# A fused QKV projection on one core: the first two row pairs dealt on even and odd rows, and the first pair's x loaded as two transfers

## The chip, the cores and the metric

The kernel runs on one core of one Trainium2 chip. The metric is device time in microseconds (us). Three runs of the kernel before gave 358.24, 358.25 and 358.67 us; their median is 358.25 us. One more execution was profiled: it took 358.3 us, and the profile covers a span of 356.5 us of it.

The engines are named as in the profile: PE is TensorE (PEld its weight loads), DVE is VectorE, ACT is ScalarE, POOL is GpSimd and SP is SyncE, which here issues most of the DMA transfers. A "q" behind a name (SPq) is that engine's sequencer.

## The reference

```python
batch, seq, hidden = 16, 512, 768
x      # (16, 512, 768)  float32
w_qkv  # (768, 2304)     float32

qkv = np.matmul(x, w_qkv)                   # (16, 512, 2304)
q, k, v = qkv[..., :768], qkv[..., 768:1536], qkv[..., 1536:]
return np.stack([q, k, v], axis=0)          # (3, 16, 512, 768)
```

Flattened, this is an 8192 x 768 matrix times a 768 x 2304 matrix, with the 2304 columns of the product cut into three outputs. 25 MB of x and 7 MB of weights are read, and 75.5 MB are written.

## The kernel before, in words

**Tiling.** The 8192 rows of x are worked through in 32 *pairs*; pair `p` holds rows 256p to 256p+255, as two row tiles of 128 rows each. The 768 inner elements are six slices `j` of 128 (`KT = 6`). The 2304 columns are two wide groups `q` of 1024 columns, each of two blocks `c` of `CB = 512`, and a remainder of 256 columns between them (`REM`). A row of x or of an output is 768 floats, which is 3072 bytes.

**Two ways to multiply.** Pairs 2 to 31 use a seven-product scheme (L234 to L291) on sums of x and sums of weights. Those sums of the weights are not there at the start, so the first two pairs (`ND = 2`) are multiplied in the plain way, in bf16, by `block` (L463 to L489), which walks over the slices `j` and, within a slice, over the four row tiles of pairs 0 and 1. The change touches only these first two pairs.

**How pairs 0 and 1 are prepared.** `load_rows(p)` (L157) loads a whole pair in one DMA transfer of 768 KB: partition m receives row m of the first tile and row 128+m of the second. `cast_row` (L168) then casts one row tile to bf16, its columns split between DVE and ACT; `turn_row` (L173) transposes it on PE into PSUM; `copy_row` (L182) copies it out of PSUM into `xb`, from which the products take their stationary operand. All other pairs come in by other loads (L125 to L145) and are transposed on DVE.

**Order of the work.** The schedule is manual: each engine runs its instructions in the order in which the code lists them. The opening is L434 to L548. SP issues, one after another: the two x loads, six weight slices of 256 KB each for block (0, 0) (L441), two transfers of 768 KB for block (0, 1), the remainder's weights, eight transfers of 96 KB for pair 2, and so on. Eight DMA semaphores are handed out in turn, so each transfer's issue waits until the transfer eight places before it has landed: the first eight are issued without a wait, and the first 768 KB transfer of block (0, 1) waits for pair 0's load, the second for pair 1's load.

PE meanwhile runs ten matmuls on a tile of zeros (`busy(10)`, L521). Then come the transposes of pair 0, two more matmuls on zeros (L527), the transposes of pair 1, and the 24 products of block (0, 0) (L541). The casts stand in the same order on DVE and ACT: both row tiles of pair 0, both row tiles of pair 1, then the weight slices. On DVE the first copy out of PSUM stands between pair 0's casts and pair 1's.

**Stores.** `rows_of(s, p, lo, hi)` (L293) gives the place of a pair in output s. `store_quad` (L296) uses it for the wide groups and `rem` (L313) for the remainder. The stores of pairs 0 and 1 are issued from L581, L584 and L626.

Of the kernel before, what the change touches and what calls it, by code (L numbers as in the profile page):

```python
# [10 lines left out]
def kernel(  # L11
# [20 lines left out]
    nc = tc.nc  # L32
    P = 128
# [6 lines left out]
    KH = KT // 2  # L40
    KC = K // 4
    NP = M // (2 * P)
    CB = 512
    REM = N3 - 4 * CB
    Q_OFF = (0, 2 * CB + REM)
    R_OFF = 2 * CB
    fp32 = mybir.dt.float32
# [6 lines left out]
    x_flat = x.rearrange("b t h -> (b t) h")  # L54
    out_flat = out.rearrange("s b t h -> s (b t) h")
# [21 lines left out]

    b1 = [w_pool.tile([P, KT, CB], bf16, name=f"b1_{q}") for q in range(2)]
    b22 = [w_pool.tile([P, KH, CB], f32r, name=f"b22_{q}") for q in range(2)]
    t_0 = w_pool.tile([P, 4, KH, CB], f32r, name="t_0")  # L80
    w_rem[1] = rem_pool.tile([P, KH, REM], bf16, name="w_rem1")
# [39 lines left out]
    xin, xf, xb, sr = {}, {}, {}, {}  # L121
# [19 lines left out]
    def load_x(p, other):  # L141
        xin[p] = xin_pool.tile([P, 2 * P // G, KC], fp32, name="xin")
        load_x_half(p, 0, nc.sync)
        if other is not None:
            load_x_half(p, 1, other)  # L145

    def transpose(p, cuts=(0, 8)):
        if p not in xf:
            xf[p] = xf_pool.tile([P, KT, 2 * P], fp32, name="xf")
        turned = xf[p][:].rearrange("p j (g b) -> p g j b", b=G)  # L150
        rows = xin[p][:].rearrange("p g (a j) -> p g j a", a=G)
        for g, end in zip(cuts, cuts[1:]):
            nc.vector.transpose(turned[:, g:end], rows[:, g:end])  # L153

    def load_rows(p):  # L157
        xin[p] = xin_pool.tile([P, 2, K], fp32, name="xin")
        rows = x_flat[p * 2 * P:(p + 1) * 2 * P, :]
        nc.sync.dma_start(xin[p][:], rows.rearrange("(r m) k -> m r k", m=P))  # L160

    xc, turned_rows = {}, {}

# [63 lines left out]
    def quad(p, q, pool=o_pool, tag="o"):  # L227
        u = Quad()
        u.p, u.q = p, q
        u.o = pool.tile([P, 2, 2 * CB], fp32, name="o", tag=tag)  # L230
        u.x = u.y = u.z = None
        return u

    def product(u, n, ps, start):  # L234
        t1, t2, t3, t4 = ts[u.q]
        if n <= 2:
            h = (n - 1) * KH
            lhs = [xb[u.p][:, h + j, :P] for j in range(KH)]
            rhs = [b1[u.q][:, h + j, :] for j in range(KH)]
        else:  # L240
            k, t = {3: (4, b22[u.q][:]), 4: (0, t4), 5: (1, t1), 6: (2, t2), 7: (3, t3)}[n]
            lhs = [sr[u.p][:, k, j, :] for j in range(KH)]
            rhs = [t[:, j, :] for j in range(KH)]
        for j in range(KH):
            nc.tensor.matmul(  # L245
                ps[:], lhs[j], rhs[j],
                start=(start and j == 0), stop=(j == KH - 1), skip_group_check=True,
            )
# [7 lines left out]
    def do(u, n, out=True):  # L256
# [17 lines left out]
        elif n == 5:  # L274
            u.y = bank()
            product(u, 5, u.y, True)
            if u.p == NP - 1:
                nc.scalar.activation(c22, u.y[:], ident)
        elif n == 7:
            product(u, 7, u.x, False)  # L280
            if u.p == NP - 1:
                nc.vector.tensor_tensor(c22, c22, u.x[:], op=add)
# [8 lines left out]
            nc.vector.tensor_tensor(c12, c12, u.y[:], op=add)  # L291

    def rows_of(s, p, lo, hi):  # L293
        return out_flat[s, p * 2 * P:(p + 1) * 2 * P, lo:hi].rearrange("(r m) n -> m r n", m=P)

    def store_quad(u):  # L296
        if u.q == 0:
            nc.sync.dma_start(rows_of(0, u.p, 0, H), u.o[:, :, :H])
            nc.sync.dma_start(rows_of(1, u.p, 0, 2 * CB - H), u.o[:, :, H:])
        else:  # L300
            part = 2 * H - Q_OFF[1]
            nc.sync.dma_start(rows_of(1, u.p, H - part, H), u.o[:, :, :part])
            nc.sync.dma_start(rows_of(2, u.p, 0, H), u.o[:, :, part:])
# [9 lines left out]
    def rem(p, eng=nc.sync, between=None):  # L313
        ps = ps_pool.tile([P, 2, REM], fp32, name="ps")
        rem_row(p, 0, ps[:, 0, :])
        if between is not None:
            between()
        rem_row(p, 1, ps[:, 1, :])

        def copied():  # L320
            o = or_pool.tile([P, 2, REM], fp32, name="orem")
            act.activation(o[:], ps[:], ident)  # L322
            return lambda: eng.dma_start(rows_of(1, p, R_OFF - H, R_OFF - H + REM), o[:])

        return copied

    def two(a, b, early, u=None):

        do(a, 1)
        do(b, 1, u is None)  # L330
        if u is None:
            early()
            rem(a.p)()()
        else:
            middle(u)
            copied = rem(a.p, between=lambda: third(u))
            evacuate(b)
            early()
            copied()()
            fourth(u)  # L340
            load_x(a.p + 3, nc.sync)
        do(a, 2)
        do(b, 2)
        summed(a, b)
# [27 lines left out]
    def plain(a, b, c, d, early, rem_c, stored=False):  # L372

        add_first(a)
        add_first(b)
        rem(a.p)()()
        do(c, 1)
        do(d, 1)
        early()
        rem_c()  # L380
        do(c, 2)
        do(d, 2)
        add_second(a)
        add_second(b)
        if stored:
            for u in (c, d):
                store_cols(u, 0, 0, CB, nc.sync)
# [43 lines left out]
        rem_stored(a.p, 1, 2, lambda dst, src: act.activation(dst, src, ident), nc.sync)  # L431


    ND = 2  # L434
    zero = xb_pool.tile([P, CB], bf16, name="zero", tag="xb")
    nc.vector.memset(zero[:], 0.0)
    load_rows(0)
    nc.scalar.activation(tiny[:], zero[:, :1], ident)
    make_identity(nc, eye)
    load_rows(1)  # L440
    load_blocks(0, 0, 1)  # L441
    load_blocks(0, 1)
# [66 lines left out]
    def ahead(p, reversed_pair):  # L509
        transpose(p)  # L510
        if reversed_pair:
            sums_x(p)
            round_x(p)
        else:
            round_x(p)
            sums_x(p)
# [114 lines left out]
    def load_next(p, other):  # L631
        if p < NP:
            load_x(p, other)

    def early():
        ahead(ND + 2, False)
        load_x(ND + 3, nc.sync)

    two(quad(ND + 1, 0), quad(ND + 1, 1), early, u2)

    def early():
        ahead(ND + 3, True)
        load_x(ND + 5, nc.sync)

    two(quad(ND + 2, 0), quad(ND + 2, 1), early)
    transpose(ND + 4, (0, 4))

    for p in range(ND + 3, NP - 1, 2):
        first = p == ND + 3
# [6 lines left out]
        def early():  # L656
            ahead(p + 2, p + 2 < NP - 1)
            load_next(p + 4, nc.scalar)
# [6 lines left out]
        c, d = quad(p + 1, 0), quad(p + 1, 1)  # L665
        final = p + 3 >= NP
        plain(a, b, c, d, early, lambda: rem(c.p)()(), final)
# [32 lines left out]
```

## Time and profile before

| what | before |
|---|---|
| median of three runs | 358.25 us |
| the profiled execution | 358.3 us |
| its span | 356.5 us |
| PE busy | 351.5 us (99%) |
| DVE / ACT / POOL busy | 264.3 / 186.0 / 177.3 us |
| DMA moved | 108.10 MB, mean 303 GB/s |
| pair 0's x landed | 5.03 us after the start of the span |
| pair 1's x landed | 6.86 us |
| first product of block (0, 0) | 8.12 us |

The chain of waits is read backwards from the last instruction, and says at each step what the work had waited for. Idle time of an engine off that chain costs nothing. Times inside the profile are counted from the start of its span. A line of the timeline gives start, duration (of a merged group, from its first start to its last end or next start), engine, line, operation, tiles, shapes, how many, and in brackets the idle time before it with what ended it. The lines of the windows give, for one stretch, busy time and number of instructions of each engine, the granted PE clock, the DMA share, and GB/s.

### The profile page before, as it was taken

How to read it: one execution, taken by the hardware profiler on the slowest of the kernel's cores; microseconds unless marked ns; L12 is line 12 of the kernel's file. 1: busy time of each engine (PE TensorE's matmuls, PEld its weight loads, DVE VectorE, ACT ScalarE, POOL GpSimd, SP SyncE). 2: the span in 40 equal slices, each digit the busy share in tenths (PEclk: the TensorE clock that was granted, in tenths of full speed). 3: DMA queues.
4: the chain of work that ended last, by engine and by line, in shares of the span. 5: the costliest groups of instructions: out<-in, count | busy, mean ns of one | idle time of the engine just before them, and what ended most of it. 6: DMA issues, size and time to landing. Idle time of an engine off the chain costs nothing.

```text
span 356.5 us, 5348 instructions
## 1 busy us (share of the span) xinstructions
PE 351.5 (99%) x1782; PEld 252.2 (71%) x1782; DVE 264.3 (74%) x309; ACT 186.0 (52%) x321; POOL 177.3 (50%) x184
## 2 busy tenths in 40 slices
PE   7999999999999999999999999999999999999996
PEld 3474677768677686877768677686877868777675
DVE  3799876796877869777695876969777696876743
ACT  4587755445454553645545454553645545454553
POOL 0121773376566453665535566353665535566320
PEclk9999999999999999999999999999999999999999
DMA  7998999999999898998979889699999989887397
GB/s 297 379 351 258 323 373 344 371 325 360 293 337 311 250 362 204 357 258 299 351 189 385 229 311 338 174 406 242 346 272 299 331 196 390 232 295 293 146 377 273
DMA packets 82075, 108.10 MB, mean 303 GB/s; under 512 B 4992, under 2 KB 62080, under 8 KB 82048
## 3 DMA queue, kind: packets, MB, share of 16 engines
q1 hardware_dynamic: 75520, 103.04, 86.2%
q10 hardware_dynamic: 6528, 4.72, 5.1%
q8 instruction: 14, 0.23, 0.3%
q14 instruction: 13, 0.11, 0.1%
HBM read 32.24 MB, written 75.50 MB: 302 GB/s over the span
## 4 chain that ended last, share of the span: by engine, by line
PE 97%; DMA 2%; ACT 0%; SPq 0%; issue 0%
PE ps L245 79%; PE ps L308 11%; PE ps L479 6%; DMA xin<-in_x_dram 2%; PE ps L412 0%; PE ps L179 0%; ACT xc L166 0%; SPq L160 0%; ACT orem L431 0%
## 5 line engine op out<-in xcount | busy, mean ns | idle before, releaser
L245 PE MATMUL ps<-t,s 128*128 128x512 f32 x720 | 178.0, 395 | 0.0
L245 PEld LDWEIGHTS ps<-t,s 128*128 128x128 f32 x720 | 135.0, 188 | 29.6
L153 DVE STREAM_TRANSPOSE xf<-xin 128x768 f32<-128x768 f32 (+2 forms) x46 | 93.4, 2033 | 2.8 <-DMA xin<-in_x_dram 2.8
L245 PE MATMUL ps<-b,xb 128*128 128x512 bf16 x360 | 85.2, 379 | 0.0
L285 DVE TENSOR_TENSOR o<-o,ps 128x512 f32<-128x512 f32 x56 | 38.5, 687 | 51.8 <-ACT o L284 51.8
L192 POOL CAST xb<-xf 128x1536 bf16<-128x1536 f32 x28 | 41.0, 1465 | 56.9 <-DVE xf L153 56.9
L212 POOL TENSOR_TENSOR s<-xf 128x384 fp32r<-128x384 f32 x29 | 31.0, 1067 | 72.9 <-DVE xf L153 71.2
L245 PEld LDWEIGHTS <-xb 128*128 128x128 bf16 x360 | 34.0, 98 | 36.9 <-issue 4.2
L291 DVE TENSOR_TENSOR o<-o,ps 128x512 f32<-128x512 f32 x60 | 41.1, 686 | 20.7 <-PE ps L245 19.5
L284 ACT ACTIVATE o<-ps 128x512 f32<-128x512 f32 x56 | 33.5, 598 | 42.1 <-PE ps L245 42.1
L245 PE MATMUL ps<-b,s 128*128 128x512 f32 x180 | 50.6, 389 | 0.0
L288 ACT ACTIVATE o<-ps 128x512 f32<-128x512 f32 x60 | 35.9, 598 | 25.2 <-PE ps L245 22.8
L365 DVE TENSOR_TENSOR o<-o,ps 128x512 f32<-128x512 f32 x78 | 47.8, 681 | 0.0
L273 ACT ACTIVATE o<-ps 128x512 f32<-128x512 f32 x60 | 36.0, 599 | 19.1 <-PE ps L245 15.4
L308 PE MATMUL ps<-w_rem,xb 128*128 128x256 bf16 x372 | 45.7, 273 | 0.0
L322 ACT ACTIVATE orem<-ps 128x512 f32<-128x512 f32 x31 | 18.5, 597 | 49.1 <-PE ps L308 28.5
L308 PEld LDWEIGHTS <-xb 128*128 128x128 bf16 x372 | 36.2, 98 | 10.9 <-issue 0.3
L245 PEld LDWEIGHTS ps<-b,s 128*128 128x128 f32 x180 | 33.8, 188 | 7.0
L213 POOL TENSOR_TENSOR s<-s,xf 128x384 fp32r<-128x384 f32 x29 | 29.5, 1018 | 2.3
L214 POOL TENSOR_TENSOR s<-xf 128x384 fp32r<-128x384 f32 x29 | 29.4, 1015 | 0.0
L216 POOL TENSOR_TENSOR s<-xf,s 128x384 fp32r<-128x384 f32 x29 | 29.2, 1008 | 0.0
L369 ACT ACTIVATE o<-ps 128x512 f32<-128x512 f32 x26 | 15.5, 598 | 16.9 <-PE ps L245 16.1
(53 smaller groups left out, 164.9 us busy)
## 6 DMA issues: line engine op xcount, KB each, us to landing
out_dram<-o SPq DMA_DIRECT2D x60, 768.0 KB, 4.7
out_dram<-o SPq DMA_DIRECT2D x76, 256.0 KB, 3.9
xin<-in_x_dram SPq DMA_DIRECT2D x88, 192.0 KB, 5.6
out_dram<-orem SPq DMA_DIRECT2D x31, 256.0 KB, 2.4
xin<-in_x_dram ACTq DMA_DIRECT2D x24, 192.0 KB, 4.4
st<-in_w_qkv_dram SPq DMA_DIRECT2D x5, 768.0 KB, 7.7
xin<-in_x_dram SPq DMA_DIRECT2D x2, 768.0 KB, 4.9
st<-in_w_qkv_dram SPq DMA_DIRECT2D x6, 256.0 KB, 6.0
```

Source lines behind the costliest of these rows:

```text
L153: nc.vector.transpose(turned[:, g:end], rows[:, g:end])
L192: nc.gpsimd.tensor_copy(out=xb[p][:], in_=xf[p][:])
L212: 1: lambda g: g.tensor_tensor(s[:, 1], a21, a22, op=add),
L213: 2: lambda g: g.tensor_tensor(s[:, 2], s[:, 1], a11, op=sub),
L245: nc.tensor.matmul(ps[:], lhs[j], rhs[j], start=(start and j == 0), stop=(j == KH - 1), skip_group_check=True,)
L273: nc.scalar.activation(c12, u.x[:], ident)
L284: nc.scalar.activation(c22, u.x[:], ident)
L285: nc.vector.tensor_tensor(c22, c22, u.y[:], op=add)
L288: nc.scalar.activation(c21, u.x[:], ident)
L291: nc.vector.tensor_tensor(c12, c12, u.y[:], op=add)
L308: nc.tensor.matmul(ps, xb[p][:, j, r * P:(r + 1) * P], w_rem[j // KH][:, j % KH, :], start=(j == 0), stop=(j == KT - 1), skip_group_check= ...
L365: dve.tensor_tensor(c, c, u.z[:], op=add)
```

## The change

The first 512 rows are dealt to pairs 0 and 1 in another way. Before, pair 0 held rows 0 to 255 and pair 1 rows 256 to 511. Now pair 0 holds the even rows of the first 512 and pair 1 the odd ones: row tile r of pair p, partition m, is row 256r + 2m + p. The loads follow this, and so do the stores, since `rows_of` uses the same mapping for these two pairs. On the HBM side, neighbouring partitions of one transfer are therefore 6144 bytes apart and no longer 3072.

Second, pair 0's x is loaded by two transfers of 384 KB, one for each row tile, in place of one transfer of 768 KB. Pair 1's is still one transfer.

```diff
+    ND = 2
...
-    def load_rows(p):
+    def dealt(rows, p):
+        return rows[:ND * 2 * P].rearrange("(r m p) n -> p m r n", m=P, p=ND)[p]
+
+    def load_rows(p, tiles=2):
         xin[p] = xin_pool.tile([P, 2, K], fp32, name="xin")
-        rows = x_flat[p * 2 * P:(p + 1) * 2 * P, :]
-        nc.sync.dma_start(xin[p][:], rows.rearrange("(r m) k -> m r k", m=P))
+        for r in range(0, 2, tiles):
+            n = slice(r, r + tiles)
+            nc.sync.dma_start(xin[p][:, n], dealt(x_flat, p)[:, n])
...
     def rows_of(s, p, lo, hi):
+        if p < ND:
+            return dealt(out_flat[s, :, lo:hi], p)
         return out_flat[s, p * 2 * P:(p + 1) * 2 * P, lo:hi].rearrange("(r m) n -> m r n", m=P)
...
-    ND = 2
     zero = xb_pool.tile([P, CB], bf16, name="zero", tag="xb")
     nc.vector.memset(zero[:], 0.0)
-    load_rows(0)
+    load_rows(0, 1)
```

SP issues one transfer more than before, so the rotation of the eight semaphores moves on by one place. What each later transfer waits for stays the same, with one exception: the sixth weight slice of block (0, 0) is now the ninth transfer, and its issue waits until the first half of pair 0 has landed. The first transfer of block (0, 1) waits for the second half of pair 0, where it waited for the whole. The order of instructions on PE, DVE, ACT and POOL is the same as before; what changes there is that the casts of pair 0's first row tile wait for the first half alone, and those of its second tile for the second half.

## The prediction, as put on record before the run

> **What bounds the kernel now.** I read the page's first parts, the chain of waits over the whole span and then for the first 9 us, the timeline of that stretch, and the DMA rates.
>
> ```profile
> span 356.5 us, 5348 instructions
> PE 351.5 (99%) x1782; PEld 252.2 (71%) x1782; DVE 264.3 (74%) x309; ACT 186.0 (52%) x321; POOL 177.3 (50%) x184
> PEclk9999999999999999999999999999999999999999
> ```
>
> PE is busy for all but 5.0 us. So little idle time is left that only two things can move the end: when the products begin, and whether a later wait opens a hole. The chain of the opening, start and length in us:
>
> ```profile
> 0.74 0.44 SPq L160
> 1.18 0.06 issue
> 1.24 5.62 DMA xin<-in_x_dram
> 6.86 0.02 issue
> 6.88 0.45 ACT xc L166
> 7.33 0.11 issue
> 7.44 0.85 PE ps L179 x12
> 8.29 0.86 PE ps L479 x4
> ```
>
> The transfer at 1.24 is pair 1's load, the second of the two that L160 issues. It lands at 6.86; its cast and its transposes follow, then the products, and from 8.29 on the whole chain is PE work without a hole up to the tail. Pair 0's load, the one that is split, is not on it. The timeline:
>
> ```profile
> 0.74 0.95 SPq L160 DMA_DIRECT2D xin<-in_x_dram  x2
> 1.19 4.01 PE L452 MATMUL ps<-zero 128*128 128x512 bf16 x10 [1.19 <-DVE zero L436]
> 1.74 5.51 SPq L92 DMA_DIRECT2D st<-in_w_qkv_dram  x8
> 5.03 0.94 ACT L166 ACTIVATE xc<-xin 128x384 bf16<-128x384 f32 x2 [2.81 <-DMA xin<-in_x_dram]
> 5.61 0.95 PE L179 MATMUL ps<-eye,xc 128*128 128x128 bf16 x12 [0.41 <-ACT xc L166]
> 6.40 0.59 PE L452 MATMUL ps<-zero 128*128 128x512 bf16 x2
> 6.88 0.78 ACT L166 ACTIVATE xc<-xin 128x288 bf16<-128x288 f32 x2 [0.91 <-DMA xin<-in_x_dram]
> 7.44 0.85 PE L179 MATMUL ps<-eye,xc 128*128 128x128 bf16 x12 [0.45 <-ACT xc L166]
> 8.12 5.34 PE L479 MATMUL ps<-b,xb 128*128 128x512 bf16 x24
> ```
>
> Pair 0 lands at 5.03, 1.85 us ahead of pair 1, and every engine that prepares it is idle again before pair 1 comes: ACT for 0.91 us. The DMA rate of the first 20 us, in slices of 0.5 us, and then three stretches of it:
>
> ```profile
> GB/s 0 0 0 12 129 307 430 406 412 406 424 424 389 406 410 397 406 414 410 406 393 410 422 401 406 410 414 399 371 391 387 385 366 312 241 241 257 216 232 311
> ```
>
> ```profile
> 4.00:5.00 1.00, 1.00 (x4) 0.28 (x2) 0.00 (x0) 0.00 (x0) 0.00 (x0) 1.00 1.02 409
> 6.50:10.50 4.00, 3.55 (x28) 1.74 (x25) 3.05 (x10) 3.32 (x9) 0.00 (x0) 1.00 1.05 405
> 14.40:15.60 1.20, 1.20 (x7) 0.57 (x6) 1.20 (x3) 1.00 (x2) 0.00 (x0) 1.00 1.08 386
> 33.00:60.00 27.00, 27.00 (x134) 17.86 (x133) 20.88 (x18) 16.79 (x32) 14.37 (x13) 1.00 1.03 345
> ```
>
> After a slow start between 1.5 and 3.0 us the transfers run at 400 to 430 GB/s and the engines are full (share 1.02 and up). So what sets pair 1's landing is the bytes queued ahead of it, 786 KB of pair 0, and its own 786 KB; the split leaves these as they are.
>
> **The change, part by part.**
>
> *One more issue on SP.* The two issues of L160 start 0.50 us apart (0.74 and 1.24), so pair 1's moves from 1.24 to 1.74, and the weights' issues, from 1.74, by 0.50 too. Cover: data began to flow about 1.2 us after the first issue (0.74 to 1.9), so pair 1's could at 2.9. Adding up the slices of 0.5 us, pair 0's 786 KB have been moved at about 4.35: 1.4 us of cover. The first weight slice is ready at 2.24 + 1.2 = 3.4, and its turn comes when 1573 KB have moved, at about 6.25. Cost 0. Without that cover it would be the 0.50 us.
>
> *The new semaphore wait.* The sixth weight slice now waits for pair 0's first half. Half of pair 0, 393 KB, has moved at about 3.4; landings lag the bytes by about 0.7 (4.35 to 5.03), so it lands at about 4.1. SP reaches that issue only at about 4.9 (five issues took 2.63 from 1.74, the sixth began at 4.41, plus 0.50). No wait, and behind it the block (0, 1) transfers wait for the same landings as before: the second half at 5.03, pair 1 at 6.86. The first of them goes out at about 5.4 where it went at 5.03, with four weight slices still queued ahead. Cost 0.
>
> *The split itself.* 16 more completion packets (the page counts 4992 packets under 512 B, 16 for each of 312 transfers). How much a boundary between transfers costs is seen in the weight slices of 262 KB: the DVE casts that wait for them start at 9.47, 10.11 and 10.81, so 0.64 to 0.70 apart, which is 374 to 410 GB/s with every boundary included, against 405 in that whole stretch. 262 KB at 424 GB/s, the best slice, would take 0.62. So a boundary costs between 0 and 0.08; I take 0.02, since the middle one is 0.66 or less against 0.65 at 405 GB/s.
>
> The Trainium skill's page "DMA: Bandwidth & Descriptors", section "Anatomy of one DMA", gives for transfers issued from GpSimd a fixed 2.0 us for each besides bytes / 436 GB/s, and its rules ask for large ones. If that were paid in turn, the second transfer would add an estimated 2.0 us on the chain. The 0.64 to 0.70 between slices says that queued transfers overlap theirs, so I don't add it.
>
> *Even and odd rows, reading.* Rows stay 3072 bytes, only their distance in HBM doubles to 6144. Rows of that length ran at 409 GB/s (4 to 5 us); weight slices, 2048 bytes every 55 KB (a partition's six rows of 9216), at 405; the remainder's weights, 1024 bytes every 9216, at 386. The rate falls with the length of the piece, not with its distance. Value 0, as it is nearest to the row of 3072 bytes. Upper end: both pairs, 1573 KB, at 386 in place of 409: 4.08 against 3.85, +0.23. Lower end: the slow start. From 1.9 to 2.6 the rate was 132, from 2.6 to 3.0 it was 330; against 418 afterwards that is (0.7 x 286 + 0.4 x 88) / 418 = 0.56 us lost. Other addresses and shorter first transfers could take away up to all of it, -0.56.
>
> *Even and odd rows, writing.* Pairs 0 and 1 write 512 x 9216 bytes = 4.7 MB, from about 21 us on, in the same pieces. Value 0. Upper end: 4.7 MB at 386 in place of 409 is 12.2 against 11.5 us, 0.7 us of DMA time, at 33 to 60 us, where the engines are full. PE is covered there: 27.00 of 27.00 busy, and it would have to wait for a buffer or an x load held back. Bounds 0 and +0.7, nearest to 0 as nothing shows PE near such a wait.
>
> *What starts earlier.* The first row tile's casts (ACT 0.94 for two, so 0.47) run from 4.1 to 4.6. Its transposes still stand behind the ten matmuls on zeros, which end at 5.20, so six of the twelve go 0.4 us sooner; the second tile's half is cast at 5.03 to 5.50 and transposed from 5.61, where the first tile's was. The two matmuls on zeros come at 6.0 and not at 6.40, and PE then idles until 7.44 as before: its hole of 0.45 grows to about 0.85. Nothing on the chain moves: ACT and DVE wait for pair 1 either way, longer. Gain 0.
>
> *Sum.* 358.3 us (span 356.5 and 1.8 around it) + 0 + 0 + 0.02 + 0 + 0 = 358.3; the profiled execution is 0.05 above the median, so the forecast stays at 358.3.
>
> **Rivals.**
>
> *The slow start shrinks* (faster). For: the rate takes 1.1 us to come up (129, 307, then 430), and the first transfer is half as long. Against: the bytes and the first issue at 0.74 are unchanged. Pair 1 and all weights behind it come 0.3 to 0.56 sooner: 357.75 to 358.0. That is still within 0.2% (0.72 us, about what a measurement of this kernel can tell from no change); only more than the whole 0.56 would pass it.
>
> *The PE clock falls back* (slower). Ten matmuls took 4.01 us before 5.2 (0.40 each), 24 took 5.34 after 8.1 (0.22): the array runs at half rate until it has been busy for a while. With one hole grown to 0.85 us it could return to half rate when the products begin: for a time like the first slow stretch, about 3.4 us (1.19 to 4.6), half the work is lost, +1.7: 360.0. It decides from the point where a hole of 0.85 suffices; two holes of 0.41 and 0.45 left the rate at 0.22. The Trainium skill, "TensorE: Matmul & The Clock Gate", section "The HAM clock gate", says that an idle window of about 3.4 us is needed; by that rule this rival is out, and no row here shows so long a hole.
>
> *The larger pitch costs* (slower): +0.23 in the opening and up to 0.7 in the stores: 358.5 to 359.2. For: engines full at 33 to 60. Against: the rates above.
>
> *The halves don't land apart*, so that nothing starts earlier: the same 358.3, since nothing that starts earlier is on the chain.
>
> **How the numbers follow.** Forecast, no change within 0.2 us (with the halves not apart): 0.60. Slow start shorter: 0.17, of which 0.06 beyond 0.72 us. Larger pitch: 0.15, of which 0.06 beyond 0.72 us. Clock: 0.05. Something unseen in the opening, slower: 0.03. So faster 0.06, same 0.80, slower 0.14. The range goes from the shorter start's 357.7 to the pitch's larger part, 359.0; it leaves out about 0.15.
>
> **What would show it.** Right: three issues for x in the opening, pair 1 landing at 6.8 to 6.95; the first cast at about 4.1 and PE's hole before pair 1's transposes near 0.85; first product at 8.1 to 8.2, 24 products in 5.3; rate 400 and up from 3 us; no new hole on PE. Wrong: pair 1's landing moved by more than 0.3 us; products at 0.40 apart after 8 us; PE idle behind a DMA between 20 and 60 us.

## The result: about 1.3 us slower, and not the same from run to run

The changed kernel takes 359.66 us, the median of 12 runs (358.60 to 362.58); the kernel before takes 358.31 in 12 runs beside them (358.24 to 358.76). The ratio is 1.0051, with a 95% interval of 1.0036 to 1.0067. The forecast was 358.3, no change. The median lies outside the range 357.7 to 359.0.

The spread is a result too. The kernel before repeats within 0.5 us, the changed one spreads over 4 us. In three of its runs (362.05, 362.15, 362.58) the mean granted PE clock was 0.995, in the other nine (358.60 to 360.88, median 359.55) 0.999 or more. The profiled execution is one of the three: 362.05 us, span 360.3, so 3.8 us of span over before. Comparisons below leave out five disturbed runs (364.56, 401.37, 737.64 and 1291.8 us of the experiments' kernels, the last with the array at a quarter of its rate, and 401.35 of the kernel before).

The page's first lines after the change:

```profile
span 360.3 us, 5330 instructions
PE 352.6 (98%) x1763; PEld 253.3 (70%) x1782; DVE 263.7 (73%) x309; ACT 186.5 (52%) x321; POOL 177.6 (49%) x184
...
PEclk9899999999999999999999999999999999999999
```

PE now lacks 7.7 us of the span where it lacked 5.0, and the second slice of the clock row shows an 8. Both the loss and the lower clock are in the opening. The chain of waits for the first 12 us, after (start, length, what):

```profile
0.74 0.39 SPq L165
1.13 0.06 issue
1.19 0.42 SPq L165
1.61 0.05 issue
1.66 7.15 DMA xin<-in_x_dram
8.80 0.02 issue
8.83 0.45 ACT xc L171
9.28 0.10 issue
9.38 0.93 PE ps L184 x12
10.32 1.71 PE ps L485 x4
```

It is the same chain through pair 1's load. The issue moved from 1.24 to 1.66, but the landing moved from 6.86 to 8.80. Pair 1's load, whose instructions the split does not touch, takes 7.15 us from issue to landing where it took 5.62. The timeline of the same stretch, after:

```profile
4.01 0.52 ACT L171 ACTIVATE xc<-xin 128x384 bf16<-128x384 f32 x1 [1.78 <-DMA xin<-in_x_dram]
...
4.91 0.52 ACT L171 ACTIVATE xc<-xin 128x384 bf16<-128x384 f32 x1 [0.37 <-DMA xin<-in_x_dram]
...
5.43 1.39 PE L184 MATMUL ps<-eye,xc 128*128 128x128 bf16 x12
...
6.66 0.59 PE L458 MATMUL ps<-zero 128*128 128x512 bf16 x2
8.83 0.78 ACT L171 ACTIVATE xc<-xin 128x288 bf16<-128x288 f32 x2 [3.40 <-DMA xin<-in_x_dram]
...
9.38 0.93 PE L184 MATMUL ps<-eye,xc 128*128 128x128 bf16 x12 [2.13 <-ACT xc L171]
...
10.11 3.74 PE L485 MATMUL ps<-b,xb 128*128 128x512 bf16 x9
```

The two halves of pair 0 do land apart, at 4.01 and 4.91 (forecast 4.1 and, as before, 5.03). Then ACT waits 3.40 us for pair 1 and PE stands idle for 2.13. The first nine products take 3.74 us, about 0.42 each, where 24 took 5.34 before (0.22). The DMA rate of the first 20 us, in slices of 0.5 us, after:

```profile
GB/s 0 0 0 74 209 338 350 399 307 320 356 344 344 283 320 352 371 397 397 410 410 389 410 410 418 401 406 414 395 389 383 391 384 367 170 224 262 236 150 78
```

Before, the rate stood between 389 and 430 from 3.0 to 14 us. Now it starts a little earlier (74, 209) but stays between 283 and 371 from 4.0 to 8.5 us. That is not a lower rate of all transfers. The trace records the landing of a load in 16 shares, which are read here as those of the 16 DMA engines: of pair 1's load 12 have landed by 6.79, and the last four land at 7.15, 7.85, 8.72 and 8.80. Before, all 16 landed within 6.34 to 6.86. Of the first weight slice behind it, 13 shares land between 7.24 and 7.91 and three at 8.49, 9.36 and 9.45, so the same few seem to lag on. Single packets of 3072 bytes, which otherwise take about 0.12 us, took up to 0.96 (before, from 3 to 9 us, at most 0.18). A few DMA engines stalled, and a load has landed only when its last engine has.

Windows of after, and then of before at the corresponding places (stretch; length, PE, PEld, DVE, ACT and POOL busy with counts; granted PE clock; DMA share; GB/s):

```profile
6.60:10.00 3.40, 1.27 (x16) 0.81 (x15) 1.25 (x5) 1.12 (x4) 0.00 (x0) 1.00 1.01 365
10.10:13.40 3.30, 3.30 (x11) 1.19 (x9) 2.21 (x6) 2.10 (x6) 0.00 (x0) 0.50 1.05 407
13.50:17.00 3.50, 3.45 (x17) 1.60 (x17) 2.36 (x4) 1.15 (x3) 0.00 (x0) 1.00 1.07 389
```

```profile
4.70:8.00 3.30, 2.44 (x27) 1.47 (x26) 2.10 (x7) 2.00 (x6) 0.00 (x0) 1.00 1.03 407
10.00:12.40 2.40, 2.40 (x13) 1.08 (x11) 0.85 (x2) 0.25 (x1) 0.00 (x0) 1.00 1.05 407
```

After, the clock is granted at 0.50 for one stretch from about 10 to 13.4 us, and at 1.00 again behind it. Before it there, PE had been busy for 1.27 of 3.40 us (37%); before the change it was busy for 2.44 of 3.30 (74%) ahead of the products, and the clock stayed at 1.00.

The account of the profiled execution, after less before: pair 1's cast starts 1.95 us later (8.83 against 6.88), the first product 1.99 later (10.11 against 8.12). The first remainder products, behind the stretch of half clock, start 3.63 later (22.11 against 18.48), and the last products of the chain too (355.83 against 352.20). So a late load costs 2.0 us, the clock another 1.6, and behind 23 us nothing is gained or lost. That the stores cost nothing is right; what is wrong lies in the opening.

### The profile page after: what moved, and what is told of

Same layout as the page of the kernel before. It is cut to its first block, busy times and chain, and to the rows that moved or that the text cites. A ratio compares the mean times of both kernels' runs of the same rounds, so it can differ in the third digit from the quotient of the medians.

```text
span 360.3 us, 5330 instructions
## 1 busy us (share of the span) xinstructions
PE 352.6 (98%) x1763; PEld 253.3 (70%) x1782; DVE 263.7 (73%) x309; ACT 186.5 (52%) x321; POOL 177.6 (49%) x184
## 4 chain that ended last, share of the span: by engine, by line
PE 74%; POOL 15%; DVE 6%; issue 2%; DMA 2%; SPq 0%; ACT 0%
PE ps L250 55%; PE ps L315 11%; PE ps L485 6%; DVE xf L154 5%; POOL xb L197 5%; POOL s L218 3%; POOL s L217 3%; POOL s L219 3%; DMA xin<-in_x_dram 2%; PE ps L419 0%; PE ps L184 0%; SPq L165 0%; DVE o L296 0%; ACT xc L171 0%; ACT orem L438 0%
## 5 line engine op out<-in xcount | busy, mean ns | idle before, releaser
L250 PE MATMUL ps<-b,xb 128*128 128x512 bf16 x343 | 81.4, 379 | 1.1
L376 ACT ACTIVATE o<-ps 128x512 f32<-128x512 f32 x26 | 15.6, 599 | 17.6 <-PE ps L250 16.9
```

The source lines that it names most:

```text
L250: nc.tensor.matmul(ps[:], lhs[j], rhs[j], start=(start and j == 0), stop=(j == KH - 1), skip_group_check=True,)
```

## The experiments

Three questions are open: which part of the change makes pair 1 land late, what about that part does it, and whether the hole on PE alone sets the clock back. All kernels were timed against the kernel before, whose median was 358.33 to 358.37 in each comparison.

### One part at a time

The expectations of the first four weigh: A, the doubled pitch of the reads slows them (A1: by itself; A2: only because two transfers read interleaved rows at the same time); B, the extra transfer in flight does it; C, the stores do it.

The split alone, with rows as before:

```diff
-    def load_rows(p):
+    def load_rows(p, tiles=2):
         xin[p] = xin_pool.tile([P, 2, K], fp32, name="xin")
         rows = x_flat[p * 2 * P:(p + 1) * 2 * P, :]
-        nc.sync.dma_start(xin[p][:], rows.rearrange("(r m) k -> m r k", m=P))
+        for r in range(0, 2, tiles):
+            n = slice(r, r + tiles)
+            nc.sync.dma_start(xin[p][:, n], rows.rearrange("(r m) k -> m r k", m=P)[:, n])
...
-    load_rows(0)
+    load_rows(0, 1)
```

> Rows as before (pair 0 is rows 0 to 255), only the first pair's x in two transfers of one row tile. Theory A, that the reads at a pitch of 6144 bytes stall the DMA: no change, 358.3 within 0.3, pair 1 lands at 6.8 to 7.0, every run at a mean clock of 1.0. Theory B, that the extra transfer in flight stalls it: as the changed kernel, 359.4 or more at the median, pair 1 landing 1 us or more late. Theory C, that it is the stores: no change, 358.3.

Measured: 360.91 us, ratio 1.0065 [1.0041, 1.0088]. The six runs fall into two groups: 358.34 and 358.47, and 360.85 to 361.81. The profiled one is the undisturbed 358.34; its chain:

```profile
1.65 5.14 DMA xin<-in_x_dram
6.79 0.02 issue
6.81 0.45 ACT xc L168
```

Where the DMA engines do not stall, pair 1's load lands at 6.79, slightly earlier than before, and the split costs nothing, as forecast. In four of six runs something takes 2.5 us or more; none of these four was profiled. So the split alone is enough for a loss as large as the whole change's, and it strikes at random.

The rows alone, pair 0 in one transfer:

```diff
 (the change, with)
-    load_rows(0, 1)
+    load_rows(0)
```

> Even and odd rows for loads and stores, but pair 0 in one transfer of 768 KB as before. Theory A (pitch of the reads): as the changed kernel, median 359.4 or more, some runs near 362 with a mean clock of 0.995, pair 1 landing after 7.3. Theory B (the extra transfer): 358.3 within 0.3. Theory C (stores): slower by up to 1 us, but with pair 1 landing at 6.9.

Measured: 359.68 us (359.25 to 360.07), ratio 1.0037 [1.0025, 1.0049]. It is slower too, but steadily. Its chain and its DMA rate:

```profile
0.74 5.14 DMA xin<-in_x_dram
5.88 0.02 issue
5.91 0.53 ACT xc L171
6.44 0.05 issue
6.48 1.48 PE ps L184 x12
7.96 0.85 PE ps L458 x2
8.82 1.24 PE ps L184 x12
...
GB/s 0 0 0 25 111 135 147 197 424 393 399 418 424 404 402 414 406 402 402 402 418 406 406 406 418 406 406 401 403 403 379 389 384 376 180 204 241 257 180 243
```

Here the chain runs through pair 0's load, which lands at 5.88 in place of 5.03. The rate is only 111 to 197 GB/s from 2.0 to 4.0 us, and full (424) from then on: the slow start, over at 3.0 us before, lasts until 4.0. There is no tail of single engines; single packets of 3072 bytes took up to 1.74 us in the first 3 us (0.58 before). PE, fed 0.85 us later, is also still at its first, slow rate: 12 transposes take 1.48 us and the two matmuls on zeros 0.85, where they took 0.95 and 0.59. The first product starts at 9.89, 1.77 later, and this execution's 360.07 is 1.77 above before's profiled 358.3. Of the 1.77, pair 1's later cast is 0.92 (7.80 against 6.88), and PE's slow rate is the rest: the trace first records the clock as full at 9.89, before at 4.62. So this is another cost than the split's: the doubled pitch slows the first transfer.

The loads of the change with the stores as before, so that the rows of pairs 0 and 1 are stored in another order than the reference's:

```diff
 (the change, without)
-        if p < ND:
-            return dealt(out_flat[s, :, lo:hi], p)
```

> Loads as in the changed kernel, stores as before, so that the first 512 rows of the output come out in another order: this part of the computation is changed. Theories A and B: as the changed kernel, median 359.4 or more, since nothing behind the opening counts. Theory C (stores): 358.3 within 0.3.

Measured: 360.68 us (358.77 to 361.45), ratio 1.006 [1.0042, 1.0079]. The loss is there without the stores' part. C falls.

The profiled run (360.21 us, clock 1.00) shows a second way in which the stalls cost. Pair 1's cast starts at 8.16, 1.28 later than before, but the run is 1.9 above it. Its chain does not pass through pair 1:

```profile
2.13 6.65 DMA st<-in_w_qkv_dram
8.79 10.52 DMA str<-in_w_qkv_dram
19.36 1.22 POOL w_rem L558
20.62 2.45 PE ps L313 x21
```

The first weight slice, queued behind pair 1, lands late too. The issue of the remainder's weights waits for that landing, so it goes out at 8.79 where it went at 7.52; they land late, their cast on POOL starts at 19.36 where it started at 16.91, and PE waits for it. By 23 us the loss has grown from 1.28 to 1.8. In the profiled run of the change PE, at half clock, had not yet come so far, and this wait did not show.

The change, but pair 1 read as 256 neighbouring rows from elsewhere (rows 512 to 767, so the output of pair 1's rows is another):

```diff
+            src = dealt(x_flat, 0) if p == 0 else x_flat[4 * P:6 * P, :].rearrange("(r m) k -> m r k", m=P)
-            nc.sync.dma_start(xin[p][:, n], dealt(x_flat, p)[:, n])
+            nc.sync.dma_start(xin[p][:, n], src[:, n])
```

> As the changed kernel, but pair 1's x is read from rows 512 to 767, contiguous, in one transfer, so that no two transfers read neighbouring rows; the products of pair 1 are then of other rows, which changes this part of the computation. Theory A1, that the pitch of 6144 bytes alone stalls the reads: pair 0 is still slow to land, pair 1 late by at least 0.5 us, median 358.8 or more. Theory A2, that two transfers in flight over interleaved rows stall each other: no stall, 358.3 within 0.3, pair 1 lands by 7.0.

Measured: 360.27 us (359.77 to 361.62), ratio 1.0059 [1.0045, 1.0072]. Its rate falls just as pair 1 is being read, from 4 us on, though pair 1's rows are neither apart nor interleaved with pair 0's:

```profile
GB/s 0 0 0 49 184 381 412 424 240 283 252 338 356 313 356 385 389 381 389 402 410 418 397 406 410 406 406 406 403 387 395 381 384 367 252 248 264 206 144 86
```

A2 falls. What is left is that two things cost: even and odd rows in the first transfer, and the split.

### What about the split?

The next expectations weigh: T1, one more transfer in flight is enough; T2, a short first transfer (later: short transfers as such); T3, the casts, which now begin at 4.0 us, collide with the loads that still write to SBUF.

Split, with the second row tile cast first, so that the first casts wait for the second half:

```diff
-    for r in range(2):
+    for r in (1, 0):
         cast_row(0, r, K // 2)
```

> As the split alone, but pair 0's second row tile is cast before its first, so no engine works on x before both halves have landed at about 4.9. Theory T1, that one more transfer in flight makes the stalls: median 359.4 or more with single runs 2 us apart. Theory T2, that a short first transfer sets all lanes on cold addresses at once: the same. Theory T3, that the early casts at 4.0 collide with the loads: 358.3 within 0.3, all runs within 0.3 of each other.

Measured: 361.46 us in five runs (360.46 to 363.45), ratio 1.009 [1.0067, 1.0113]. The early casts are gone and the loss is not. T3 falls.

A transfer of 128 x 4 bytes ahead of whole loads:

```diff
+    probe = w_pool.tile([P, 1], fp32, name="probe")
+    nc.sync.dma_start(probe[:], x_flat[M - P:, :1])
     load_rows(0)
```

> The kernel before with one more transfer in front, 128 x 4 bytes of x into a spare tile, and both pairs' x whole. T1 (one more transfer): median 359.4 or more with spread. T2 (short first transfer on cold addresses): about 358.8, pair 1 later by the 0.5 us of the issue at most, little spread. T3 (early casts): as T2.

Measured: 365.18 us (364.7 to 365.7), ratio 1.0191 [1.0177, 1.0204]. This does not answer the question: the chain of waits of this run passes between 52 and 84 us through stores and x loads of 6.5 to 9.3 us, far behind the opening. The added tile has moved every later tile in SBUF by 4 bytes per partition. That would fit: over the whole run SP's queue kept the DMA engines busy for 90.9% of the span, before for 86.2%, and in the later run with an added tile behind all others for 86.2% again. The shift by itself was not tried.

Pair 0 split by columns: two transfers, each with half of the columns of both row tiles:

```diff
-        nc.sync.dma_start(xin[p][:], rows.rearrange("(r m) k -> m r k", m=P))
+        for c in range(0, K, K // 2 * tiles):
+            n = slice(c, c + K // 2 * tiles)
+            nc.sync.dma_start(xin[p][:, :, n], rows.rearrange("(r m) k -> m r k", m=P)[:, :, n])
```

> Rows as before, pair 0's x in two transfers, by halves of the columns (pieces of 1536 bytes) and not by row tiles, so that the casts wait for both. T1 and T2: median 359.4 or more with spread. T3 (early casts): 358.3 to 358.6, no spread.

Measured: 360.29 us, ratio 1.0047 [1.0027, 1.0067]; of 12 runs four at 358.38 to 358.73, eight at 359.68 to 361.8. It is the same loss with the same two groups, whichever way pair 0 is cut. About T3 it says less than was expected. DVE casts just the first half of the columns, and in the profiled run its casts start at 3.96, ahead of the second half, which lands at 5.63; only ACT's wait until 5.65.

Pair 0 whole, pair 1 split:

```diff
     load_rows(0)
...
-    load_rows(1)
+    load_rows(1, 1)
```

> Rows as before, pair 0 whole, pair 1 in two transfers of one row tile. T1 (one more transfer in flight): median 359.4 or more with spread. T2 (short first transfer): 358.3 within 0.3 or a little less, since pair 1's first half is there 0.9 us sooner but its second is not; no spread. T3 (early casts of pair 0): the same as T2.

Measured: 358.92 us (358.32 to 359.51), ratio 1.0016 [1.0007, 1.0025]. Most of the loss is gone, though transfers and bytes are as many. In the profiled run the second half landed at 7.12. So it matters that the two short transfers come first.

The extra transfer again, in front of whole loads, as 128 x 512 bytes and in a tile behind all others:

```diff
+    probe = probe_pool.tile([P, 128], fp32, name="probe")
+    nc.sync.dma_start(probe[:], x_flat[M - P:, :128])
     load_rows(0)
```

> The kernel before with one more transfer in front, 128 x 512 bytes of x into a spare tile that lies behind all others, so that no other tile moves; both pairs whole. T1 (one more transfer in the queue makes the stalls): median 359.4 or more, runs spread over 1 us or more, stalls at 4 to 6 us in the profile. T2 (what counts is that pair 0 itself comes in short transfers): 358.8 at most, 0.5 us being the issue put in front, runs within 0.3 of each other.

Measured: 359.01 us (358.85 to 359.33 in nine of ten runs, 360.37 in the tenth), ratio 1.0022 [1.0013, 1.0031]. Pair 1's cast starts at 7.37, 0.49 later than before, which is about one issue of SP. A third transfer in flight costs no more than its issue in nine of ten runs, and does not split them into two groups. T1 falls. An issue ahead of pair 0's load is paid in full, then, where the prediction's issue between pair 0's and pair 1's is covered.

The second half issued by ACT, the rest as in the split alone:

```diff
-            nc.sync.dma_start(xin[p][:, n], rows.rearrange("(r m) k -> m r k", m=P)[:, n])
+            (nc.scalar if r else nc.sync).dma_start(xin[p][:, n], rows.rearrange("(r m) k -> m r k", m=P)[:, n])
```

> Rows as before, pair 0 in two transfers of one row tile, the second issued by ACT on its own queue, so that SP issues no more transfers than before. T1 (the number on SP's queue): 358.3 within 0.3, little spread. T2 (short transfers as such): as the split alone, median 360 or more, spread of 2 us.

Measured: 358.31 us (358.18 to 358.55 in nine runs), ratio 0.9999 [0.9989, 1.0008]. Its chain and rate:

```profile
1.19 5.44 DMA xin<-in_x_dram
6.63 0.02 issue
6.65 0.45 ACT xc L168
...
GB/s 0 0 0 111 233 344 412 393 387 412 381 403 381 414 401 397 397 402 410 406 406 410 406 410 410 406 410 393 377 389 383 385 363 287 238 252 242 249 268 373
```

Pair 1 lands at 6.63, the rate does not sag, and none of the nine is late. The same two halves of the same bytes, queued on two engines, cost 2.6 us less in the median than both queued on SP (358.31 against 360.91). Short transfers as such are therefore not the cause either. Two things differ besides the queue, and this run does not separate them: the halves move side by side and land at 4.67 and 4.84, nearly together, and SP issues pair 1's load at 1.19 and not at 1.65. So this is no test of the step *What starts earlier*. The undisturbed profile of the split alone is one: there the halves land at 4.00 and 4.91, and at 358.34 us nothing is gained.

The Trainium skill, "DMA: Bandwidth & Descriptors", section "Issuing engines are not separate DMA queues", says that issuing from several engines saves only the issue time, as all share the same DMA engines. The full rate agrees (about 405 GB/s in both), the landings at the start do not: by that rule this run would differ from the split alone by an estimated one issue, 0.4 us, and it differs by 2.6 in the median. The measurement decides here.

The split alone with the weights behind it in two transfers of 768 KB and not six of 256 KB:

```diff
-    load_blocks(0, 0, 1)
+    load_blocks(0, 0, 3)
```

> Rows as before, pair 0 in two transfers as in the split alone, but block (0, 0)'s weights in two transfers of 768 KB and not six of 256 KB, so that SP has five transfers queued ahead of block (0, 1) where it had nine. If the number of transfers queued behind the loads makes the stalls: pair 1 lands by 7.0 in every run and the runs lie within 0.4 of each other, at about 359 to 359.6, since the first slice of weights now comes with two others, 1.3 us later. If two short transfers of pair 0 in a row are enough: spread of 2 us, runs at 360 to 363.

Measured: 364.29 us (362.71 to 364.61), ratio 1.0157 [1.0139, 1.0176]. Larger weight transfers have a price of their own (a first product at 11.05 and a clock at half for two stretches), but the question was pair 1: its cast starts at 8.69, as late as in the change. How many transfers are queued behind the two halves is not what makes it late.

### Even and odd rows, by themselves

The change with the second half issued by ACT, which takes the split's damage away:

```diff
-            nc.sync.dma_start(xin[p][:, n], dealt(x_flat, p)[:, n])
+            (nc.scalar if r else nc.sync).dma_start(xin[p][:, n], dealt(x_flat, p)[:, n])
```

> The changed kernel, with the second half of pair 0 issued by ACT on its own queue. If the even and odd rows cost nothing by themselves and only short transfers in a row on SP's queue stall: 358.3 within 0.3. If the even and odd rows slow the first loads whoever issues them: 359.0 to 360, pair 1 landing at 7.3 or later, the rate below 200 GB/s until 3 us or more.

Measured: 359.36 us (358.77 to 359.59), ratio 1.0025 [1.0015, 1.0035]. What is left, 1.0 us, is steady, and lies in the start of the rate (the profiled run is the fastest of the nine, with pair 1 landing at 7.21):

```profile
GB/s 0 0 0 55 160 221 313 406 406 424 399 412 420 385 418 406 406 406 401 406 406 414 406 406 414 410 406 406 381 383 393 385 367 296 220 237 266 197 204 89
```

It reaches 400 at 3.5 us and stays there. The same kernel with neighbouring rows (the one before it with ACT's issue) reached 412 at 3.0 us, and pair 1 landed at 6.63.

The kernel before, with pair 1 alone read from every second row (the even rows of 512 to 1023, so pair 1's output is another):

```diff
+        if p == 1:
+            rows = x_flat[4 * P:8 * P, :].rearrange("(r m p) k -> p m r k", m=P, p=2)[0]
```

> The kernel before, both loads whole and pair 0 as before; pair 1's x is read from the even rows of rows 512 to 1023, so that the products of pair 1 are of other rows and this part of the computation is changed. If a pitch of 6144 bytes is slow wherever it comes: pair 1 lands 0.2 or more late, 358.5 to 359.7. If it costs only in the first transfer, while the loads start: 358.3 within 0.2.

Measured: 358.59 us (358.37 to 358.95), ratio 1.0007 [0.9997, 1.0016]: no difference that can be told, 0.26 us by the medians. Pair 1's cast starts at 6.92, against 6.88. So the pitch of 6144 bytes costs next to nothing in a transfer that comes second, and in the very first one 1.0 to 1.3 us in the median, with what follows from it.

### The hole and the clock

The kernel before with five casts on DVE ahead of pair 1's (they repeat a cast of pair 0 and change no value). Loads are untouched, but pair 1 comes late to PE:

```diff
+    for _ in range(5):
+        dve.tensor_copy(out=xc[0][:, 0, :480], in_=xin[0][:, 0, :480])
     (pair 1's casts)
```

> The kernel before, its loads untouched, with five more casts of 0.4 us on DVE ahead of pair 1's, so that pair 1's transposes start about 1.7 us later and PE's hole grows from 0.45 to about 2.1. If a hole of that length can set the clock back: start +1.7 and in some runs, or all, another 1.7 for a stretch at half rate: 360.0, or 361.7 with a mean clock of 0.995. If it needs a hole of 3.4: 360.0 within 0.3 in every run, clock 1.0.

Measured: 361.63 us, ratio 1.0078 [1.0062, 1.0093]. Two of six runs are at 360.02 and 360.15 with a clock of 1.00, four at 361.57 to 361.73 with 0.995. PE's timeline in one of the four, and its windows:

```profile
6.42 0.59 PE L452 MATMUL ps<-zero 128*128 128x512 bf16 x2
...
9.12 1.46 PE L179 MATMUL ps<-eye,xc 128*128 128x128 bf16 x12 [2.11 <-DVE xc L165]
10.37 2.94 PE L479 MATMUL ps<-b,xb 128*128 128x512 bf16 x8
```

```profile
5.70:9.00 3.30, 1.31 (x14) 0.80 (x14) 2.66 (x8) 1.35 (x4) 0.00 (x0) 1.00 1.05 407
9.10:12.40 3.30, 3.28 (x17) 2.03 (x18) 2.46 (x9) 2.27 (x6) 0.00 (x0) 0.50 1.05 408
12.50:16.00 3.50, 3.50 (x18) 1.61 (x17) 3.31 (x6) 0.63 (x1) 0.00 (x0) 1.00 1.06 393
```

Here a hole of 2.11 us, with PE busy 40% of the 3.3 us before (1.31 / 3.30), was followed by one stretch at half clock. Two of six runs go without it, and the two groups are 1.6 us apart: this is the price of the clock, and it equals the 1.6 of the result's account.

The length of the hole alone does not decide. In the profiled runs of two experiments above PE stood idle for longer, and the clock stayed at 1.00. The loads without the stores' part (a line of PE's timeline, then two windows), and pair 1 from elsewhere:

```profile
8.72 0.85 PE L184 MATMUL ps<-eye,xc 128*128 128x128 bf16 x12 [2.31 <-ACT xc L171]
3.85:7.26 3.41, 2.27 (x19) 1.16 (x17) 1.05 (x3) 1.05 (x2) 0.00 (x0) 1.00 1.00 381
7.27:10.68 3.41, 1.96 (x18) 1.25 (x19) 2.14 (x7) 2.47 (x8) 0.00 (x0) 1.00 1.04 393
```

```profile
8.89 0.85 PE L185 MATMUL ps<-eye,xc 128*128 128x128 bf16 x12 [2.57 <-ACT xc L172]
4.44:7.85 3.41, 1.88 (x17) 1.05 (x15) 0.72 (x2) 0.53 (x1) 0.00 (x0) 1.00 0.95 319
7.85:11.26 3.41, 2.37 (x20) 1.45 (x21) 2.51 (x8) 2.88 (x9) 0.00 (x0) 1.00 1.05 397
```

The windows are not chosen freely. The traces record when the granted clock changed, and within each trace these times lie 3.41 us, or a whole multiple of it, apart. Where this grid lies differs from execution to execution: the clock is first recorded as full at 4.62 us before, at 6.60 in the changed kernel, at 5.65 with the hole alone, at 3.85 and 4.44 here. With the hole inside one stretch of the grid PE was busy for 37 to 40% of it, and half clock followed: the changed kernel, the hole alone, and the fewer weight transfers (1.33 of 3.41). Here an edge of the grid falls into the hole, PE is busy for 55% or more of each stretch, and nothing follows. So in these five traces it was PE's busy share of one stretch that went with the clock, and a hole of 2 us could cost 1.6 us or nothing by where the grid lay. No run set that place, and none shows where between 40 and 55% the limit is.

The change with twelve matmuls on zeros in place of two ahead of pair 1's transposes:

```diff
-    busy(2)
+    busy(12)
```

> The changed kernel with twelve matmuls on zeros in place of two between the transposes of pair 0 and pair 1, 2.2 us more of PE work that fills the hole. If the runs near 362 come from the clock falling back in that hole: no run with a mean clock of 0.995, all between 359.3 and 361, median 359.8. If they come from the loads alone: runs at 362 and more remain.

Measured: 360.42 us (359.68 to 361.7), ratio 1.0059 [1.0044, 1.0074]. None of six runs has the lower clock; at three in twelve without the fill, six runs are few. The run of 361.7 was profiled: pair 1's cast starts at 9.36 there, 2.48 later than before, and PE then waits 0.27 and 0.19 us for the casts of the remainder's weights: late loads alone can cost 3 us. No run with the fill shows the clock's part; but the load's lateness differs from run to run by more than that, and the medians (360.42 here, 359.66 for the change) show no gain.

## Why the prediction was wrong

Of the signs of being wrong that the prediction names, two appear in the profiled run: pair 1 landed 1.94 us later, and products ran at about 0.42 us each after 8 us.

*One more issue on SP*: right as to this issue. It put 0 against a cover of 1.4 us; where the split was undisturbed the time was before's (358.34 and 358.47, against 358.37).

*The new semaphore wait*, *Even and odd rows, writing*, *What starts earlier*: right for an undisturbed split. The loss stood without the changed stores, nothing behind 23 us added to it, and the undisturbed split gained nothing (358.34). With the stalls, the old waits for landings pass the delay on: the remainder's weights go out 1.3 to 2.5 us late, a wait that the first of these steps did not follow to its end. Of the hole on PE the third step said 0.85 and was too high. In the undisturbed run of the split alone it is 0.51, since the ten matmuls on zeros end at 5.64 there and not at 5.20 (full clock from 5.76, before from 4.62); the 2.13 of the changed kernel come from the late load.

*The split itself* is the first step that failed. It priced the boundary between transfers at 0 to 0.08 us, from weight slices that were queued one behind another at full rate. The boundary is that cheap, as the undisturbed runs show. What the step had no term for is that two short transfers at the head of SP's queue make single DMA engines stall a little later (single packets took up to 1.36 us in these profiles), so that the *next* load, on the chain, lands 0 to 2.5 us late in the profiled runs. In the split alone, with what follows from it, that came to 2.5 us in the median.

*Even and odd rows, reading* is the second. "The rate falls with the length of the piece, not with its distance" was read from transfers between 4 and 15.6 us, already running. For a transfer that comes second it held within what can be told (358.59). For the first transfer it did not: 1.0 to 1.3 us with what follows, against an upper end of 0.23. The step did look at the slow start, but only as something to gain (-0.56); it should have carried the same row as a bound above, since nothing in the trace said which way other addresses would move it.

*The PE clock falls back* had the right mechanism and price (1.7 forecast, 1.6 measured), and the wrong condition: it was tied to a hole of 0.85 us, and the hole became 2.1 because another step failed; and what went with the clock was PE's busy share of a stretch of 3.41 us, not the hole's length alone. A loss that needs a further loss ahead of it should have had its chance worked out together with that one. The rule that put it out, an idle window of about 3.4 us (the Trainium skill, "TensorE: Matmul & The Clock Gate", "The HAM clock gate"), does not agree with these runs if it is read as a fully idle window: in the profiled ones 2.1 us idle and 37 to 40% busy in the last 3.3 to 3.4 us sufficed. The same section says that the window runs freely and does not start with the kernel. The traces agree: their grid of 3.41 us starts at another place in each execution, and holes of 2.31 and 2.57 us with an edge of it inside cost no clock.

*The larger pitch costs* ended on the right side of the forecast for a cause it had not given, and its 358.5 to 359.2 ends below the median.

The sizes do not add up in the changed kernel: split alone +2.5, rows alone +1.3, both +1.3 in the median. With even and odd rows split on SP, the start is quicker than with one transfer (74 and 209 in the fourth and fifth slice, against 25 and 111), and the stalls come on top in some runs. With two causes of which one strikes at random, five to twelve runs fix each median only to about 0.6 us.

**What stays open.** Why a few DMA engines stall after two short x loads on SP's queue. It is not the count of transfers, not short transfers issued from two queues, not the early casts, the stores, the rows' distance or the transfers behind them; no run looked further inside. Also open is why the first transfer alone minds the distance of its rows, and what decides where the clock's grid lies.

## What to carry to other kernels

A rate read from the middle of a trace says nothing about the first transfers of a kernel: give those their own bounds, on both sides, and look at several executions, since a load that lands late in half of them does not show in one. A part that is off the chain can still disturb the transfer that is on it; if an early load has to be cut in two, put the halves on two queues (where they landed nearly together here, so that nothing came much earlier), and see whether what comes earlier is waited for at all (here it was not). Count PE's holes in the opening together with what may lengthen them: one of 2.1 us cost another 1.6 us of clock where it fell into one stretch of the clock's grid.

## What was not expected of the hardware

- Two loads of 384 KB at the head of one queue stalled single DMA engines in part of the runs, with packets of 3072 bytes taking up to 0.96 us in the changed kernel in place of 0.12; a median of 360.91 us against 358.31 with one of them on ACT's queue.
- Rows 6144 bytes apart slowed the first transfer (111 to 197 GB/s until 4.0 us), and the second one not measurably.
- The array's clock fell to 0.50 for 3.41 us after a hole of 2.1 us with PE busy 37 to 40% of the stretch before (the mean clock shows it in 4 of 6 runs with such a hole and unchanged loads); after holes of 2.31 and 2.57 us split over two stretches, with PE busy 55% or more in each, it did not.
- A tile of 4 bytes per partition ahead of all others, with a transfer of 512 bytes, cost 6.8 us (365.18 against 358.34), along a chain through stores and x loads at 52 to 84 us; its cause was not isolated.
